# Norm sums, sums' engine, bias rows, last stores and last output chunk of an encoder trunk

## The chip, the cores and the metric

One core of a Trainium2 chip runs the whole program. The metric is device time in microseconds (us), the median of three runs. Everything is 32-bit float at the interface. The engines are TensorE (PE; PEld is its weight load), VectorE (DVE), ScalarE (ACT), GpSimd (POOL) and SyncE (SP, which issues most transfers). Each has a queue of its own and works it off in order.

## The reference

A trunk of two layers on `x` of 1024 tokens by 1024 features. Layer 0 is chunkwise retention (4 heads), layer 1 is chunked attention (16 heads of 64, each chunk of 64 queries sees itself and 8 chunks before it, with a learned relative bias), and each is followed by a squared-ReLU MLP of width 4096. Cut to what matters:

```python
for i in range(DEPTH):                       # 2
    hn = _rmsnorm(h, mix_norm_g[i])          # h * rsqrt(mean(h*h) + eps) * gain
    h = h + (_retention if i == 0 else _chunk_attention)(hn, ...)
    u = relu(_rmsnorm(h, mlp_norm_g[i]) @ mlp_w1[i])
    h = h + (u * u) @ mlp_w2[i]
return _rmsnorm(h, final_norm_g)
# attention, per chunk and head
s = q @ k.T * scale + bias[max(rel, -256) + 256]
o = softmax(s) @ v                            # then o @ att_w_out
```

## The kernel before, in words

The activations `h` stay in the core's memory, turned: 8 tiles of 128 features by 1024 tokens, worked in two halves (`hf`) of 512 tokens. Every full-precision product is made of three single-pass ones: an operand is split into a rounded high half (ScalarE) and the rest as a low half (VectorE), by `split` (L133), and `mm3` (L159) issues high x high, low x high, high x low.

**Norms.** A projection runs on `h` times the gain, not yet divided by the root mean square; that factor is applied to the outputs. `Norm.square` (L203) squares a tile on ScalarE and GpSimd adds it to one of two accumulators `acc`. `Norm.finish` (L219) then splits `acc` into `ah` and `al` on VectorE, lets TensorE sum over the partitions with matmuls against two columns of ones (`pc`), computes the inverse root (`col_rsqrt`), and, where the factor is wanted along the columns, writes it 128 wide on VectorE (`wide`), has TensorE turn it and ScalarE copy it to `rB`.

**Seven products.** The up projections of both MLPs and the projections of the attention layer (`Seven`, 16, 12 and 16 jobs of 256 output columns) use seven block products in place of eight (Strassen-Winograd). `XNorm.block` (L284) makes the operands of products 1, 2, 5, 6 while the projection before still runs; `late` (L304) makes those of 3, 7, 4 during the first products. `Group.sums` (L331) makes four sums of weight blocks on GpSimd per job, `make` splits a weight into halves. `Seven.go` (L392) issues a list of steps (job, product): products 1, 2, 5, 6 of jobs 0 and 1, then 3, 3, 7, 4, 7, 4, then the jobs one after the other. Each step gets its weights ready two steps ahead; behind each step an evacuation on VectorE or ScalarE follows and `done` scales an output by `rB` and stores it. Hooks by step number hang in the norm (`finish` of half 0 behind step 0, of half 1 behind step 1) and the late operands (`spread`, L418). The text calls the first 14 steps a start.

**Attention layer.** `qk_job` (L959) scales a tile of queries or keys, splits it and stores four pieces through SyncE (L974); `bias_rows` (L1022) builds, behind step 15, a table of the bias rows, all from ScalarE's queue, and sends 16 rows, each to 64 rows of a skewed copy (L1034 to L1036). The core loads heads (`load_q`, `load_k`, `load_b`, L1049 to L1069) and runs 64 units (head, group of queries) as a software pipeline of scores, softmax, transposes and values. Beside it a `Filler` issues a group of the output projection per unit: `att_out` (L1079) takes chunks of 256 rows of the output weights, three of them beside the core, the fourth behind it (L1230), where `XNorm.block` follows each finished tile.

**Orders.** The framework lays out each engine's queue from the order in the code and from what is ready in its plan; pools of tiles whose memory is reused wait tile by tile. At the start of the program (L666 to L683) the squares of both halves, two projections, `finish` of half 0 and the first rotary products follow one another; half 1 comes inside the second pair. At its end (L1259 to L1285) the final norm's squares, `finish` and the stores of the output are interleaved with the last products.

```python
def finish(self, psp, hf, row=True):
    ah = self.own("ah", F32R)
    al = self.own("al", F32R)
    split(self.acc[hf], ah, al, "dve")
...
hooks[0].append(lambda: fin(0))
hooks[1].append(lambda: fin(1))
```

## Time and profile before

| | |
|---|---|
| median of 3 runs | 2930.65 us (2927.86 to 2933.59) |
| the profiled execution, its own time | 2939.48 us |
| its span, first to last instruction | 2937.7 us |
| mean granted TensorE clock over the span | 0.972 |
| busy: TensorE, VectorE, ScalarE, GpSimd | 95%, 54%, 36%, 23% |
| memory traffic | 313 MB, 107 GB/s |

The rows of the next section come from one profiled execution. Times are from the span's start. A wait row reads "who, at which line, for whom: us in total, times, longest". A group row reads "line, engine, operation, output and inputs, shapes, count, then busy us, mean ns of one, then idle time of the engine just before". A timeline row reads "start, duration, engine, line, operation, output and inputs", with the idle time before it in brackets; "ACTq" and "SPq" are transfers that the engine issues.

### The profile page before, as it was taken

How to read it: one execution, taken by the hardware profiler on the slowest of the kernel's cores; microseconds unless marked ns; L12 is line 12 of the kernel's file. 1: busy time of each engine (PE TensorE's matmuls, PEld its weight loads, DVE VectorE, ACT ScalarE, POOL GpSimd, SP SyncE). 2: the span in 40 equal slices, each digit the busy share in tenths (PEclk: the TensorE clock that was granted, in tenths of full speed). 3: DMA queues.
4: the chain of work that ended last, by engine and by line, in shares of the span. 5: the costliest groups of instructions: out<-in, count | busy, mean ns of one | idle time of the engine just before them, and what ended most of it. 6: DMA issues, size and time to landing. Idle time of an engine off the chain costs nothing.

```text
span 2937.7 us, 34754 instructions
## 1 busy us (share of the span) xinstructions
PE 2783.1 (95%) x12762; PEld 2283.6 (78%) x12762; DVE 1584.8 (54%) x2659; ACT 1065.0 (36%) x1888; POOL 678.6 (23%) x591
## 2 busy tenths in 40 slices
PE   7999999889998999999999789979997999999998
PEld 6888888778886788878888568768985788788887
DVE  4331123366557744454555856668889544545544
ACT  4101221233324444431223434468874444422222
POOL 4220000032214422200001522245545322100002
PEclk9999999989999999999999899989998999999999
DMA  4322333343211233242331255586530323333321
GB/s 123 107 94 78 108 111 99 130 136 108 80 51 29 86 112 111 97 162 82 108 104 43 58 173 160 143 212 157 146 88 22 125 102 114 126 118 108 108 83 58
DMA packets 247771, 313.04 MB, mean 107 GB/s; under 512 B 14664, under 2 KB 170416, under 8 KB 245552
## 3 DMA queue, kind: packets, MB, share of 16 engines
q1 hardware_dynamic: 246048, 307.87, 33.9%
q10 hardware_dynamic: 1552, 2.95, 0.3%
q8 instruction: 100, 1.64, 0.2%
q14 instruction: 71, 0.58, 0.1%
HBM read 222.64 MB, written 90.74 MB: 107 GB/s over the span
## 4 chain that ended last, share of the span: by engine, by line
PE 81%; DVE 9%; ACT 4%; DMA 2%; issue 2%; POOL 2%; ACTq 0%; SPq 0%; POOLq 0%; DVEq 0%
PE ps L165 17%; PE ps L164 17%; PE ps L166 17%; PE pA L164 5%; PE pA L165 5%; PE pA L166 5%; PE pC L166 2%; PE pC L165 2%; PE pC L164 2%; PE po L1170 1%; DVE xl L140 1%; PE pt L1158 1%; PE pB L165 1%; PE pB L166 1%; PE pB L164 1%
## 5 line engine op out<-in xcount | busy, mean ns | idle before, releaser
L482 DVE TENSOR_TENSOR h<-ps,h 128x512 f32<-128x512 f32 x368 | 252.5, 688 | 341.6 <-PE ps L166 340.7
L136 ACT CAST whi<-wraw 128x1024 fp32r<-128x1024 f32 x132 | 138.8, 1052 | 767.4 <-PE ps L165 580.4
L165 PE MATMUL ps<-ul,whi 128*128 128x512 f32 x960 | 374.2, 390 | 1.9 <-DVE ul L140 1.7
L166 PE MATMUL ps<-uh,wlo 128*128 128x512 f32 x960 | 373.5, 389 | 0.0
L164 PE MATMUL ps<-uh,whi 128*128 128x512 f32 x960 | 373.0, 389 | 0.0
L164 PE MATMUL pA<-xh,wh 128*128 128x512 f32 x704 | 282.3, 406 | 17.0 <-ACT xh L136 5.6
L166 PE MATMUL pA<-xh,wl 128*128 128x512 f32 x704 | 281.1, 400 | 15.9 <-DVE wl L140 15.9
L165 PE MATMUL pA<-xl,wh 128*128 128x512 f32 x704 | 281.0, 399 | 5.0 <-DVE xl L140 5.0
L212 POOL TENSOR_TENSOR acc<-acc,sq 128x512 f32<-128x512 f32 x70 | 99.1, 1417 | 768.5 <-ACT sq L211 767.4
L140 DVE TENSOR_TENSOR wlo<-wraw,whi 128x1024 fp32r<-128x1024 f32 x125 | 159.2, 1274 | 171.0 <-ACT whi L136 171.0
L165 PEld LDWEIGHTS ps<-ul,whi 128*128 128x128 f32 x960 | 180.2, 188 | 42.1 <-DVE ul L140 4.5
L164 PEld LDWEIGHTS ps<-uh,whi 128*128 128x128 f32 x960 | 180.0, 188 | 37.5 <-ACT uh L136 0.4
L166 PEld LDWEIGHTS ps<-uh,wlo 128*128 128x128 f32 x960 | 180.2, 188 | 37.1
L164 PE MATMUL ps<-hhi,whi 128*128 128x512 f32 x512 | 204.5, 399 | 2.6 <-ACT whi L136 1.8
L165 PE MATMUL ps<-hlo,whi 128*128 128x512 f32 x512 | 204.3, 399 | 0.0
L166 PE MATMUL ps<-hhi,wlo 128*128 128x512 f32 x512 | 203.8, 398 | 0.0
L164 PEld LDWEIGHTS pA<-xh,wh 128*128 128x128 f32 x704 | 135.6, 193 | 59.4 <-DVE c L413 15.8
L140 DVE TENSOR_TENSOR wl<-wS,wh 128x512 fp32r<-128x512 f32 x176 | 142.5, 810 | 67.0 <-ACT wh L136 66.1
L166 PEld LDWEIGHTS pA<-xh,wl 128*128 128x128 f32 x704 | 135.0, 192 | 47.6 <-DVE wl L140 18.9
L165 PEld LDWEIGHTS pA<-xl,wh 128*128 128x128 f32 x704 | 135.5, 193 | 33.3 <-DVE xl L140 5.8
L340 POOL TENSOR_TENSOR wS<-wr 128x512 f32<-128x512 f32 x44 | 59.9, 1361 | 415.2 <-DVE wl L140 393.1
L136 ACT CAST wh<-wS 128x512 fp32r<-128x512 f32 x176 | 109.4, 621 | 123.0 <-PE pB L165 58.2
(227 smaller groups left out, 6084.9 us busy)
## 6 DMA issues: line engine op xcount, KB each, us to landing
wr<-in_mlp_w_dram SPq DMA_DIRECT2D x32, 1024.0 KB, 5.4
uD<-c SPq DMA_DIRECT2D x128, 256.0 KB, 2.0
wraw<-in_mlp_w_dram SPq DMA_DIRECT2D x64, 512.0 KB, 3.4
xr<-uD SPq DMA_DIRECT2D x128, 256.0 KB, 3.1
wraw<-in_ret_w_in_dram SPq DMA_DIRECT2D x48, 512.0 KB, 4.1
kk<-kA SPq DMA_DIRECT2D x32, 512.0 KB, 8.3
wr<-in_att_w_in_dram SPq DMA_DIRECT2D x12, 1024.0 KB, 5.3
vS<-t SPq DMA_DIRECT2D x32, 256.0 KB, 2.0
```

The costliest lines, as they stand in the source:

```text
L136: nc.scalar.copy(out=hi, in_=src)
L140: eng.tensor_tensor(out=lo, in0=src, in1=hi.bitcast(F32), op=ALU.subtract)
L164: nc.tensor.matmul(ps, lhsT=lh, rhs=rh, start=start, stop=False, skip_group_check=more)
L165: nc.tensor.matmul(ps, lhsT=lh, rhs=rl, start=False, stop=False, skip_group_check=more)
L166: nc.tensor.matmul(ps, lhsT=ll, rhs=rh, start=False, stop=stop, skip_group_check=more)
L212: nc.gpsimd.tensor_tensor(out=self.acc[hf], in0=self.acc[hf], in1=sq, op=ALU.add)
L340: nc.gpsimd.tensor_tensor(out=t, in0=a[1, 0], in1=a[0, 0], op=ALU.subtract)
L482: nc.vector.tensor_tensor(out=hv, in0=ps, in1=hv, op=ALU.add)
L1158: nc.tensor.transpose(pt[:, c - done:c - done + P], pr[:, (kb - k0) * P:(kb - k0 + 1) * P], ident)
L1170: nc.tensor.matmul(po[:, oc:oc + n], lhsT=T[hd, "v"][:, kb, :], rhs=t[:, off[kb]:off[kb] + n], start=i == 0, stop=i == len(seq) - 1)
```

## The change

The squares are added on VectorE, and so are the four sums of weight blocks. `finish` is cut in two: `sums` takes the sum over the partitions straight from the 32-bit accumulator with 4 matmuls a half, without splits, and `turn` makes `rB`, with ScalarE writing the wide rows. In `Seven.go` both `sums` stand behind step 2 and both `turn` behind step 4; outputs of earlier steps are kept and handed to `done` after step 4. The operand of product 7 is made from the tiles by ScalarE and one VectorE instruction, that of product 4 by two VectorE instructions. At the program's start `sums` of both halves come ahead of the second pair of weights, `turn` and the first rotary products inside it. The 16 bias rows leave ScalarE's queue: SyncE sends one behind every second step from 24 to 54. The stores of the last query and the last key job (32 of them) are issued by GpSimd. The output projection is cut into two chunks of 256 rows beside the attention core and one of 512 rows behind it, instead of three and one of 256.

```diff
@@ -209,31 +209,29 @@
                 nc.scalar.activation(sq, hv, AF.Square)
-                nc.gpsimd.tensor_tensor(out=self.acc[hf], in0=self.acc[hf], in1=sq, op=ALU.add)
+                nc.vector.tensor_tensor(out=self.acc[hf], in0=self.acc[hf], in1=sq, op=ALU.add)
         def block(self, m, hf):
...
             self.square(m, hf)
-        def finish(self, psp, hf, row=True):
-
-            ah = self.own("ah", F32R)
-            al = self.own("al", F32R)
-            split(self.acc[hf], ah, al, "dve")
+        def sums(self, psp, hf):
+
             pc = psp.tile([P, HT], F32, name="pc", tag="ps")
             for t in range(4):
-                for i, z in enumerate((ah, al)):
-                    nc.tensor.matmul(pc[:, 2 * t:2 * t + 2], lhsT=z[:, t * P:(t + 1) * P], rhs=ones[:, 0:2], start=i == 0, stop=i == 1)
+                nc.tensor.matmul(pc[:, 2 * t:2 * t + 2], lhsT=self.acc[hf][:, t * P:(t + 1) * P], rhs=ones.bitcast(F32)[:, 0:2], start=True, stop=True)
             col_rsqrt(self.gp, pc, hf)
-            if row:
-                wide = tmp_tile(self.gp, "wide")
-                ps = psp.tile([P, HT], F32, name="pss", tag="ps")
-                for t in range(4):
-                    sl = slice(t * P, (t + 1) * P)
-                    nc.vector.tensor_scalar(out=wide[:, sl], in0=ones.bitcast(F32), scalar1=rcol[:, 4 * hf + t:4 * hf + t + 1], scalar2=None, op0=ALU.mult)
-                    nc.tensor.transpose(ps[:, sl], wide[:, sl], ident)
-                nc.scalar.copy(out=rB[:, hf * HT:(hf + 1) * HT], in_=ps)
+
+        def turn(self, psp, hf):
+
+            wide = tmp_tile(self.gp, "wide")
+            ps = psp.tile([P, HT], F32, name="pss", tag="ps")
+            for t in range(4):
+                sl = slice(t * P, (t + 1) * P)
+                nc.scalar.activation(wide[:, sl], ones.bitcast(F32), AF.Copy, scale=rcol[:, 4 * hf + t:4 * hf + t + 1])
+                nc.tensor.transpose(ps[:, sl], wide[:, sl], ident)
+            nc.scalar.copy(out=rB[:, hf * HT:(hf + 1) * HT], in_=ps)
@@ -308,15 +306,20 @@
                 yield
-            for p, z in ((7, 0), (4, 1)):
-                for j in range(4):
-                    g, b = self.parts(j)
-                    src, q = (b[0][1], 3) if p == 7 else (b[1][0], 6)
-                    t = tmp_tile(gp, "t")
-                    nc.vector.scalar_tensor_tensor(out=t, in0=src, scalar=g[z], in1=x.hi[q][:, j, :].bitcast(F32), op0=ALU.mult, op1=ALU.subtract)
-                    nc.gpsimd.tensor_tensor(out=t, in0=t, in1=x.lo[q][:, j, :].bitcast(F32), op=ALU.subtract)
-                    x.split(p, j, t)
-                    yield
+            for j in range(4):
+                g, b = self.parts(j)
+                b22, t3 = tmp_tile(gp, "b22"), tmp_tile(gp, "t3")
+                nc.scalar.activation(b22, b[1][1], AF.Copy, scale=g[1])
+                nc.vector.scalar_tensor_tensor(out=t3, in0=b[0][1], scalar=g[0], in1=b22, op0=ALU.mult, op1=ALU.subtract)
+                x.split(7, j, t3)
+                yield
+            for j in range(4):
+                g, b = self.parts(j)
+                t4 = tmp_tile(gp, "t4")
+                nc.vector.scalar_tensor_tensor(out=t4, in0=b[1][0], scalar=g[1], in1=x.hi[6][:, j, :].bitcast(F32), op0=ALU.mult, op1=ALU.subtract)
+                nc.vector.tensor_tensor(out=t4, in0=t4, in1=x.lo[6][:, j, :].bitcast(F32), op=ALU.subtract)
+                x.split(4, j, t4)
+                yield
     class Group:
@@ -333,13 +336,13 @@
                 if p == 5:
-                    nc.gpsimd.tensor_tensor(out=t, in0=a[1, 0], in1=a[1, 1], op=ALU.add)
+                    nc.vector.tensor_tensor(out=t, in0=a[1, 0], in1=a[1, 1], op=ALU.add)
                 elif p == 6:
-                    nc.gpsimd.tensor_tensor(out=t, in0=self.s[5], in1=a[0, 0], op=ALU.subtract)
+                    nc.vector.tensor_tensor(out=t, in0=self.s[5], in1=a[0, 0], op=ALU.subtract)
                 elif p == 7:
-                    nc.gpsimd.tensor_tensor(out=t, in0=a[1, 0], in1=a[0, 0], op=ALU.subtract)
+                    nc.vector.tensor_tensor(out=t, in0=a[1, 0], in1=a[0, 0], op=ALU.subtract)
                 else:
-                    nc.gpsimd.tensor_tensor(out=t, in0=a[0, 1], in1=self.s[6], op=ALU.subtract)
+                    nc.vector.tensor_tensor(out=t, in0=a[0, 1], in1=self.s[6], op=ALU.subtract)
         def make(self, p):
@@ -351,7 +354,8 @@
-        AHEAD = 2
+
+        AHEAD, NORM = 2, 4
         def __init__(self, wa, jobs):
@@ -389,10 +393,10 @@
                 self.ready(s)
-        def go(self, wr, psp, gp, x, hooks=None):
+        def go(self, wr, psp, gp, x, hooks):
             self.wr = wr
             names = {1: "A", 2: "B", 5: "C"}
-            held = {}
+            held, pending = {}, []
             for s, (i, p) in enumerate(self.steps):
@@ -411,16 +415,21 @@
                     nc.vector.tensor_tensor(out=t, in0=bank, in1=held[i, {2: 1, 7: 5, 3: 6}[p]], op=ALU.add)
-                    done(*{2: (0, 0), 7: (1, 1), 3: (0, 1)}[p], t)
-                for f in (hooks or {}).get(s, ()):
+                    pending.append((done, *{2: (0, 0), 7: (1, 1), 3: (0, 1)}[p], t))
+                for f in hooks.get(s, ()):
                     f()
-
-    def spread(norm, xb, fin, more=()):
+                if s >= self.NORM:
+                    for f, *z in pending:
+                        f(*z)
+                    pending.clear()
+
+    def spread(norm, xb, psp, more=()):
         gen = norm.late(xb)
         hooks = {s: [] for s in range(12)}
-        hooks[0].append(lambda: fin(0))
-        hooks[1].append(lambda: fin(1))
+        for hf in range(2):
+            hooks[2].append(lambda hf=hf: norm.sums(psp, hf))
+            hooks[Seven.NORM].append(lambda hf=hf: norm.turn(psp, hf))
         for i in range(12):
@@ -534,7 +543,7 @@
             psp = pool(st, "psU", None, 2, PSUM)
-            seven.go(wr, psp, norm.gp, norm.x, spread(norm, xb, lambda hf: norm.finish(psp, hf)))
+            seven.go(wr, psp, norm.gp, norm.x, spread(norm, xb, psp))
     SEATS = 13
@@ -669,17 +678,16 @@
             first[1] = [up_group(psp, norm, w, 1) for w in ws]
-            norm.finish(psp, 0)
-            rope_scale(0)
-            rope(0, 0, *first[0])
+            norm.sums(psp, 0)
+            norm.sums(psp, 1)
             for i in range(1, 2 * RH):
...
                     p1, p2 = (up_group(psp, norm, w, hf) for w in ws)
-                    if i == 1 and hf == 0:
-                        norm.finish(psp, 1)
-                        rope_scale(1)
-                        rope(0, 1, *first[1])
+                    if i == 1:
+                        norm.turn(psp, hf)
+                        rope_scale(hf)
+                        rope(0, hf, *first[hf])
                     rope(i, hf, p1, p2)
@@ -971,7 +979,7 @@
                 for y, part in ((0, hi.bitcast(F32)), (1, t)):
-                    DMA.dma_start(out=dst[p][a, y, :, sl] if which == 0 else dst[p][a, :, y, sl], in_=part[rows, :])
+                    (nc.gpsimd if i == 3 else DMA).dma_start(out=dst[p][a, y, :, sl] if which == 0 else dst[p][a, :, y, sl], in_=part[rows, :])
         c0 = which * D + i * 2 * P
@@ -1031,11 +1039,14 @@
             nc.scalar.dma_start(out=extd[:, 639:640], in_=ext2[0:AH, 320:321])
-            for i in range(AH):
-                row = extd[i:i + 1, :]
-                nc.scalar.dma_start(out=skew[i][:, 0:640], in_=bass.AP(tensor=row.tensor, offset=row.offset, ap=[[0, DH], [1, 640]]))
-
-        seven.go(wr, psp, gp, norm.x, spread(norm, xb, lambda hf: norm.finish(psp, hf), [(15, bias_rows)]))
+
+        def skew_row(i):
+            row = extd[i:i + 1, :]
+            DMA.dma_start(out=skew[i][:, 0:640], in_=bass.AP(tensor=row.tensor, offset=row.offset, ap=[[0, DH], [1, 640]]))
+
+        more = [(15, bias_rows)] + [(24 + 2 * i, lambda i=i: skew_row(i)) for i in range(AH)]
+
+        seven.go(wr, psp, gp, norm.x, spread(norm, xb, psp, more))
     xs.close()
@@ -1073,12 +1084,11 @@
             load_b(hd)
-        NC = 2
         obuf = {}
-        def att_out(box, c, lo_eng="dve"):
-            return down(box, I["att_w_out"][0, c * NC * P:(c + 1) * NC * P, :], NC,
-                        lambda kb, hf: tuple(t[:, hf * HT:(hf + 1) * HT] for t in obuf[c * NC + kb]), "act", lo_eng)
+        def att_out(box, c0, n, lo_eng="dve"):
+            return down(box, I["att_w_out"][0, c0 * P:(c0 + n) * P, :], n,
+                        lambda kb, hf: tuple(t[:, hf * HT:(hf + 1) * HT] for t in obuf[c0 + kb]), "act", lo_eng)
         with ExitStack() as st:
@@ -1198,8 +1208,8 @@
                     j = i - L2 + 1
-                    if j % (8 * NC) == 0 and j < n:
-                        fill.add(att_out(dict(psp=pF), j // (8 * NC) - 1, "pool"))
+                    if j in (16, 32):
+                        fill.add(att_out(dict(psp=pF), j // 8 - 2, 2, "pool"))
                 if L1 <= i < n + L1:
@@ -1217,7 +1227,7 @@
             norm = XNorm(3, gp, xa, xt, 4)
-            run_tail(att_out(dict(psp=psp, norm=norm), NP // NC - 1), 8, seven)
+            run_tail(att_out(dict(psp=psp, norm=norm), NP - 4, 4), 8, seven)
         rs.close()
@@ -1267,10 +1277,10 @@
                             if m == 1:
-                                fin.finish(psp, 0, row=False)
+                                fin.sums(psp, 0)
                             elif m >= 3 and m < 7:
                                 leave(m - 3)
-                fin.finish(psp, 1, row=False)
+                fin.sums(psp, 1)
                 for t in range(4, NB):
```

## Rows read from the trace of the kernel before

**Rows 1.** The page's first part: busy us, share of the span, instructions.
```profile
PE 2783.1 (95%) x12762; PEld 2283.6 (78%) x12762; DVE 1584.8 (54%) x2659; ACT 1065.0 (36%) x1888; POOL 678.6 (23%) x591
```
**Rows 2.** Stretches: length, busy us (count) PE PEld DVE ACT POOL, clock, DMA, GB/s.
```profile
0.00:75.00 75.00, 58.56 (x263) 47.34 (x264) 35.57 (x70) 31.75 (x51) 33.79 (x31) 0.91 0.41 126
935.80:1003.30 67.50, 52.36 (x198) 40.43 (x197) 59.06 (x77) 28.23 (x52) 35.28 (x23) 0.82 0.20 57
1010.00:1235.00 225.00, 225.00 (x984) 183.47 (x983) 107.80 (x164) 96.07 (x165) 62.58 (x46) 1.00 0.33 111
1622.40:1695.70 73.30, 51.53 (x204) 38.71 (x204) 62.91 (x86) 29.40 (x52) 35.40 (x23) 0.88 0.27 72
1700.00:1735.00 35.00, 23.84 (x101) 18.38 (x101) 13.86 (x26) 8.36 (x18) 6.46 (x5) 0.80 0.60 184
...
2193.90:2216.40 22.50, 22.05 (x98) 17.95 (x98) 19.42 (x25) 12.74 (x23) 9.37 (x7) 1.00 0.15 48
2216.40:2296.40 80.00, 55.60 (x201) 41.71 (x202) 69.11 (x91) 36.49 (x64) 41.62 (x27) 0.77 0.20 63
```
**Rows 3.** Waits of TensorE, whole span; `pss` in 0 to 75 alone.
```profile
PE pc L227 <- DVE ah L138: 24.3, 4, 9.8
...
PE pS L1129 <- DMA kk<-kA: 14.6, 1, 14.6
PE pB L164 <- ACT wh L136: 11.4, 2, 11.2
...
PE pss L235 <- DVE wide L234: 7.5, 2, 5.8
```
**Rows 4.** Groups of VectorE, 930 to 1004; the last row 2300 to 2500.
```profile
L140 DVE TENSOR_TENSOR wl<-wS,wh 128x512 fp32r<-128x512 f32 x9 | 10.3, 1144 | 0.1
L140 DVE TENSOR_TENSOR xl<-t,xh 128x512 fp32r<-128x512 f32 x8 | 10.0, 1245 | 2.9 <-ACT xh L136 2.4
L316 DVE SCALAR_TENSOR_TENSOR t<-h,gall,xh 128x512 f32<-128x512 f32 x8 | 7.9, 1004 | 0.0
L266 DVE SCALAR_TENSOR_TENSOR xl<-h,gall,xh 128x512 fp32r<-128x512 f32 x6 | 7.6, 1276 | 1.8 <-ACT xh L265 1.8
...
L140 DVE TENSOR_TENSOR al<-acc,ah 128x512 fp32r<-128x512 f32 x2 | 2.4, 1224 | 0.0
L234 DVE TENSOR_SCALAR wide<-ones,rcol 128x128 f32<-128x128 f32 x8 | 1.8, 283 | 0.1
...
L140 DVE TENSOR_TENSOR wl<-wr,wh 128x512 fp32r<-128x512 f32 x31 | 21.3, 687 | 22.0 <-ACT wh L136 22.0
```
**Rows 5.** A group of GpSimd, the whole span.
```profile
L212 POOL TENSOR_TENSOR acc<-acc,sq 128x512 f32<-128x512 f32 x70 | 99.1, 1417 | 768.5 <-ACT sq L211 767.4
```
**Rows 6.** Timeline of ScalarE, 1713 to 1724.
```profile
1713.57 10.21 ACTq L1036 DMA_DIRECT2D skew<-extd  x16
1723.82 0.37 ACT L989 CAST vt<-pv 128x256 fp32r<-128x256 f32 x1 [15.76 <-DMA skew<-extd]
```
**Rows 7.** Timeline of SyncE, 1916.5 to 1917.9.
```profile
1916.66 0.59 SPq L974 DMA_DIRECT2D kA<-c  x1
1917.36 0.53 SPq L1052 DMA_DIRECT2D qh<-qA  x1
```
**Rows 8.** The page's transfers: engine, count, KB each, us to landing.
```profile
kk<-kA SPq DMA_DIRECT2D x32, 512.0 KB, 8.3
```
**Rows 9.** Stretches, the units' sums (L1178) alone: length, DVE busy (count), clock, DMA.
```profile
1945.00:1993.00 48.00, 5.88 (x14) 1.00 0.77 194
2010.00:2180.00 170.00, 16.83 (x40) 1.00 0.54 140
```
**Rows 10.** Timeline, 2918 to 2929: GpSimd's last square, VectorE's read of the sums.
```profile
2922.26 1.50 POOL L212 TENSOR_TENSOR acc<-acc,sq 128x512 f32<-128x512 f32 x1 [1.86 <-ACT sq L211]
...
2927.44 0.16 DVE L182 TENSOR_SCALAR vc<-pc 128x4 f32<-128x4 f32 x1 [2.49 <-PE pc L227]
```
**Rows 11.** Stretch 43 to 45, the sum matmuls (L227) alone: length, PE, PEld, clock.
```profile
43.00:45.00 2.00, 0.95 (x8) 1.04 (x8) 1.00 0.80 238
```

## The prediction

> **What bounds the kernel now.** The page's first part comes first: TensorE is busy 95% of the span, VectorE 54% [rows 1]. So the question is where TensorE stands still or runs at its lower level. The table of stretches tells that [rows 2]. In a steady stretch (1010 to 1235) 984 matmuls take 225 us, 0.229 us each, at a granted clock of 1.00. One product of a projection (4 blocks of 3 matmuls) is then 2.75 us, a job of seven 19.2 us. The three starts of a seven-product projection look different. Each start is the 14 products of the first two jobs, 168 matmuls, 38.5 us at the steady pace, and they took 67.5, 73.3 and 80.0 us with clocks of 0.82, 0.88 and 0.77. VectorE is busy 59.1 of 67.5, 62.9 of 73.3 and 69.1 of 80.0 us there: in these stretches it, not TensorE, is the bound. The waits of TensorE name the rest [rows 3]: 24.3 us for the split of the norm sum (`ah`), 7.5 us in the first stage for `wide`, 11.4 us for a weight half behind ScalarE, 14.6 us for the first keys of the attention core. GpSimd's own work is short, but VectorE's instructions beside it are long: a low half made from a GpSimd sum means 1144 ns in the first start, one made straight from the loaded weights in a steady stretch 687 ns [rows 4].
>
> **The change part by part.** The sum is made against the profiled execution (2939.48 us, span 2937.7); the median of the runs, 2930.65, is 8.8 us below it, and I take the sum off the median.
>
> *Additions on VectorE, in the starts.* In the first start GpSimd has 23 instructions [rows 2]: 11 weight sums, 4 squares, 8 subtractions of the late operands. Of the subtractions four disappear (product 7 now takes ScalarE's `b22`), four move. So 19 x 0.69 = 13.1 us come to VectorE. What leaves: the stretching, (1144-687)x9 + (1245-687)x8 + (1004-687)x8 + (1276-687)x6 = 14.7 us, if no GpSimd instruction runs beside it; the splits of the norm sum, 2.4 us for `al`, and 1.8 us for `wide`, which goes to ScalarE [rows 4]. 59.1 + 13.1 - 14.7 - 4.2 = 53.3 us. VectorE idled 8.4 us of that start; the ends are none of this idle time left and all of it, so 53.3 to 61.7 us. I take half, 57.5: the idle time came partly from GpSimd's answers, but ScalarE's are still awaited. First start: **-10 us** (-6 to -14). The second by the same 5.8 us on VectorE: 57.1 busy, half of 10.4 idle, 62.3: **-11 us** (-6 to -16). The wait for `ah` (9.8 us in the longest case, part of the 24.3) lies inside these sums and isn't counted again: the sums now stand behind the third product, when the squares are done, and the output of product 2 is held back to step 4. What is late next is VectorE's own queue: late operands and weight halves.
>
> *Squares before a start* are hidden by TensorE's down projection, one group of 12 matmuls (2.75 us) each; they cost 14 x 0.69 = 9.7 us of VectorE there against the stretching that leaves. Zero, between -2 and +3 us per start, is inside the ends above. *The weight sums in the steady stretch*: 46 GpSimd instructions become 46 x 0.69 = 31.7 us more on VectorE, 107.8 + 31.7 = 140 of 225 us [rows 2]. The free 38% hide them, and sums are issued two products ahead; if that cover goes, see the second rival. The pending outputs hold one 128x512 tile for three products, behind which nothing waits.
>
> *First stage.* The norm sums of both halves run ahead of the next weights and the rows are turned a projection later. The 7.5 us of waits for `wide` go [rows 3]; I take **-7 us**, since the rotary products now pile up behind `turn` (-4 to -9, the upper end for part of the 0.91 clock).
>
> *Norm sums without splits*: 4 f32 matmuls a half instead of 8. Eight took 0.95 us [rows 11]; no row shows an f32 one that isn't a transpose. Bounds: half of it, and four times that half, -0.5 to +0.95 us a half; I take 0, as the starts are VectorE's. The page FP8 and Floating Point Precision of the Trainium skill (TensorE Precision Notes) says that true FP32 takes four passes through the array, which speaks against this part; by it each half would cost the 0.95 us more, on the path in three halves (two in the first stage, one at the end), and the sum would be 59 instead of 62.
>
> *Bias rows.* ScalarE is taken for 16.4 us: it waits for the row table to land and then issues 16 transfers in 10.21 us, and the next conversion starts at 1723.82 [rows 6]. TensorE waits 11.4 us for it [rows 3]. The stretch 1700 to 1735 has 101 matmuls, at most 23.1 us of work [rows 2]: loss 11.9 us. The three table stores stay on ScalarE, but it no longer waits for them to land. On SyncE each row costs some 0.6 us, one in two products (5.5 us), steps 24 to 54, long after the table landed; the weight load and the stores behind it are later by 0.6 us at most, with whole jobs of slack. **-12 us** (-10 to -14).
>
> *Last stores on GpSimd's queue.* Now the loads of the first heads stand behind the last key stores on SyncE: the last is issued at 1916.66, the first load at 1917.36 [rows 7], and the keys take 8.3 us to land [rows 8], so TensorE waits 14.6 us. With the stores gone from SyncE, queries and keys of head 0 can go when their memory is free, products before the end; a part overlaps the last weights and waits for them. What remains is between nothing and one full landing, 8.3 us; I take 5.5, nearer the landing, as the bias tile comes last: **-9 us** (-6 to -13). GpSimd's price isn't in the trace: bounds 0.59 us (SyncE's issue [rows 7]) and 1.42 us (a 128x512 instruction of its own [rows 5]), 32 x that = 19 to 45 us, against 38.5 us of the last two jobs in which GpSimd now has nothing else. At the upper end it lags 7 us, and behind its stores stand the bias tiles' edges and the scaling of the first softmax rows; that takes the term to -3.
>
> *Last output chunk 512 deep.* One filler chunk leaves the attention core. 14 units without filler took 48 us, 3.43 each; 40 units with it 170 us, 4.25 each [rows 9]. Sixteen units lose 0.82 us each; the last four have no scores beside them, so 12 x 0.82 = 10 us (5 to 13). The chunk's 96 matmuls come back at the end: that projection grows from 96 to 192 matmuls, 43.9 us instead of 22.5. In return its blocks finish in fours instead of in two bursts, as ahead of the first start. So 22.5 + 80.0 becomes 43.9 + 57.5 = 101.4, 1 us less. Together **-11 us** (+4 to -17).
>
> *End.* From the last square's addition (2922.26, 1.50 us on GpSimd) to the sums read at 2927.44 [rows 10]: the addition is 0.8 us shorter and the split goes: **-2 us** (0 to -4).
>
> Sum: 10 + 11 + 7 + 12 + 9 + 11 + 2 = 62 us. 2930.65 - 62 = **2869 us**. All upper ends give -87, 2844; all lower ones -25 (6 + 6 + 4 + 10 + 3 - 4 + 0), 2906.
>
> **The rivals.** *VectorE's order eats the starts.* In each start its queue keeps all its idle time and the third start gains nothing net: 6 + 6 + 7 + 12 + 9 + 0 + 2 = 42, about 2889. For it: it is the bound there, and each square must wait for ScalarE. Against: the stretched rows. 0.2.
> *Sums in VectorE's queue block the weights everywhere (slower).* A sum waiting for its weights to land, or for one of three buffers, now holds up every low half and output behind it; GpSimd could wait alone. Place: each of the 44 jobs. It decides from 62/44 = 1.4 us of TensorE wait a job; at 2 us it gives 88 - 62 = +26, 2957. Against: 38% of VectorE free and sums two products ahead. 0.05.
> *GpSimd's stores hold the attention core.* If a store costs the upper price or more, the entry gains nothing: 53, 2878. The page SBUF — State Buffer of the Trainium skill (the "DVE blocks DMA" trap) says that a transfer issued from GpSimd stands while VectorE works in a two-port mode, since its descriptors can't be written; no transfer from GpSimd is in this trace. 0.12.
> *Clock and waits feed each other.* If the starts run without long waits, the 0.77 to 0.88 clocks go too and VectorE idles less: 2848. For it: clock 1.00 in every stretch without waits. 0.13.
> *The change does little of what it says*, the instructions being laid out so that the sums stay where VectorE is late: all lower ends, 2906. 0.05.
>
> **How the numbers follow.** My forecast has 0.45. All cases but one are below 2925, the bound at which 0.2%, about what a measurement of this kernel can tell from no change, begins. Faster 0.93, within 0.2% 0.02, slower 0.05. The range 2840 to 2902 holds the forecast with its terms mixed, the first, third and fourth rival; outside are the slower rival, the one that does little, and a few combinations.
>
> **What would show it.** Right: no TensorE wait of over 2 us for the norm sums; the starts at 55 to 63 us, with mean VectorE low halves near 0.69 us; no gap near the bias rows; some 5 us ahead of the core; heads 12 to 15 nearer 14 us than 17. Wrong: a steady job over 19.5 us with waits for `wl` or `wS`; GpSimd's queue still issuing stores when the first scores are done; the third start as long as before with 44 us ahead of it.

## The result and the profile after

The changed kernel takes **2858.34 us** (median of 4 runs, 2852.08 to 2860.36), the kernel before 2929.26 beside it (4 runs): ratio 0.9754, 95% interval 0.9733 to 0.9776, 71 us less. Forecast were 62 less, 2869, in a range of 2840 to 2902. The profiled execution of the changed kernel took 2858.98 us (span 2857.2), close to its median. That of before lies 10 us above the median beside it, so a difference of the two traces says some 10 us too much.

The page's first part, for [rows 1]:

```profile
PE 2763.7 (97%) x12762; PEld 2272.0 (80%) x12762; DVE 1624.3 (57%) x2851; ACT 1080.7 (38%) x1932; POOL 305.1 (11%) x351
```

GpSimd has 240 instructions fewer and VectorE 192 more, yet VectorE's busy time grew by only 39.5 us. Next the stretches, for [rows 2] (columns as there): the first stage, the first start, a steady stretch, the second start, the rest of that projection, the last output projection, the third start. From here on a start is counted exactly, from its first matmul to the first one of the third job; so counted, the three starts before were 66.4, 70.7 and 78.1 us long.

```profile
0.00:75.00 75.00, 65.48 (x313) 53.65 (x314) 41.43 (x75) 35.26 (x60) 16.69 (x17) 1.00 0.46 141
924.10:976.10 52.00, 45.77 (x193) 36.11 (x192) 42.86 (x77) 29.31 (x57) 0.00 (x0) 0.90 0.29 91
1000.00:1225.00 225.00, 225.00 (x985) 183.65 (x984) 137.39 (x212) 95.34 (x163) 0.00 (x0) 1.00 0.31 106
1596.50:1651.60 55.10, 47.38 (x193) 36.85 (x192) 45.95 (x83) 29.18 (x57) 0.00 (x0) 0.88 0.33 89
1651.60:1854.80 203.20, 201.77 (x904) 162.50 (x903) 141.94 (x237) 83.76 (x157) 15.87 (x27) 1.00 0.61 175
2120.00:2163.80 43.80, 43.80 (x196) 36.29 (x196) 35.28 (x54) 24.09 (x40) 0.73 (x1) 1.00 0.09 25
2163.80:2218.30 54.50, 47.57 (x194) 37.77 (x192) 44.01 (x78) 31.24 (x59) 0.00 (x0) 0.87 0.27 87
```

To be seen: the first stage holds 50 more matmuls in its first 75 us and has its full clock; each start is 14 to 24 us shorter; the steady stretch holds the same work with VectorE at 137.39 of 225 us; and in the starts VectorE now has 9 to 10 us without work. The waits of TensorE over the whole span, for [rows 3]:

```profile
...
PE pS L1139 <- DMA kk<-kA: 9.3, 1, 9.3
PE pA L164 <- ACT wh L136: 9.3, 3, 4.1
PE pA L166 <- DVE wl L140: 8.5, 3, 2.9
...
PE pC L164 <- ACT wh L136: 2.3, 3, 1.2
PE pc L223 <- DVE acc L212: 2.3, 1, 2.3
```

The 24.3 us for `ah`, the 7.5 for `wide` and the 11.4 for a weight half are gone. The 2.3 us for a norm sum (`acc`) stand at the program's end, none in a start. What is left in each start is a short wait at product 5 (`pC`) and two at the third job's first product. The groups of VectorE in the first start, for [rows 4]:

```profile
L140 DVE TENSOR_TENSOR wl<-wS,wh 128x512 fp32r<-128x512 f32 x8 | 5.5, 684 | 1.9 <-ACT wh L136 1.9
L140 DVE TENSOR_TENSOR xl<-t,xh 128x512 fp32r<-128x512 f32 x8 | 5.5, 683 | 0.0
L264 DVE SCALAR_TENSOR_TENSOR xl<-h,gall,xh 128x512 fp32r<-128x512 f32 x4 | 3.0, 744 | 0.1
```

They were 1144, 1245 and 1276 ns. The entry to the attention core, for [rows 7, 8]: GpSimd's last store and SyncE's load of the first keys, in the timelines of the two.

```profile
1858.70 0.52 POOL L982 DMA_DIRECT2D kA<-c  x1
```

```profile
1850.08 0.41 SPq L1063 DMA_DIRECT2D qh<-qA  x1
1855.03 1.33 SPq L1069 DMA_DIRECT2D kk<-kA  x2
```

A store costs GpSimd 0.52 us. The queries are loaded before the projection has ended (1854.8); the keys' load waits for the last product, whose memory it takes, and lands 9 us later. And the end, for [rows 10]: the last addition and VectorE's read of the sums, 1.9 us apart, 5.2 before.

```profile
2844.98 0.69 DVE L212 TENSOR_TENSOR acc<-acc,sq 128x512 f32<-128x512 f32 x1 [0.69 <-ACT sq L211]
...
2846.88 0.16 DVE L182 TENSOR_SCALAR vc<-pc 128x4 f32<-128x4 f32 x1 [0.81 <-PE pc L223]
```

### The profile page after: what moved, and what is told of

It reads as the page before. It is cut to its first block, busy times and chain, and to the rows that moved or that the text cites. A ratio compares the mean times of both kernels' runs of the same rounds, so it can differ in the third digit from the quotient of the medians.

```text
span 2857.2 us, 34484 instructions
## 1 busy us (share of the span) xinstructions
PE 2763.7 (97%) x12762; PEld 2272.0 (80%) x12762; DVE 1624.3 (57%) x2851; ACT 1080.7 (38%) x1932; POOL 305.1 (11%) x351
## 4 chain that ended last, share of the span: by engine, by line
PE 86%; DVE 6%; ACT 4%; issue 2%; DMA 1%; POOL 0%; SPq 0%; POOLq 0%; DVEq 0%; ACTq 0%
PE ps L165 18%; PE ps L164 18%; PE ps L166 18%; PE pA L164 6%; PE pA L166 5%; PE pA L165 5%; PE pC L164 3%; PE pC L166 3%; PE pC L165 3%; PE pB L164 1%; PE pB L166 1%; PE pB L165 1%; PE po L1180 1%; PE pt L1168 1%; ACT pr L1148 1%
## 5 line engine op out<-in xcount | busy, mean ns | idle before, releaser
L491 DVE TENSOR_TENSOR h<-ps,h 128x512 f32<-128x512 f32 x352 | 242.2, 689 | 343.3 <-PE ps L166 342.3
L164 PE MATMUL pC<-xh,wh 128*128 128x512 f32 x352 | 139.8, 397 | 2.3 <-ACT wh L136 2.3
L166 PE MATMUL pC<-xh,wl 128*128 128x512 f32 x352 | 140.4, 399 | 0.6 <-DVE wl L140 0.6
L140 DVE TENSOR_TENSOR wl<-wS,wh 128x512 fp32r<-128x512 f32 x176 | 120.9, 687 | 33.6 <-ACT wh L136 33.0
```

The source lines that it names most:

```text
L140: eng.tensor_tensor(out=lo, in0=src, in1=hi.bitcast(F32), op=ALU.subtract)
L164: nc.tensor.matmul(ps, lhsT=lh, rhs=rh, start=start, stop=False, skip_group_check=more)
L166: nc.tensor.matmul(ps, lhsT=ll, rhs=rh, start=False, stop=stop, skip_group_check=more)
L491: nc.vector.tensor_tensor(out=hv, in0=ps, in1=hv, op=ALU.add)
```

## The experiments

All but the first take the changed kernel and undo or move one part, e5, e11 and e12 two; each was timed in turn with the kernel before (2929 to 2930 us).

| run | median us | ratio to before, 95% | the three starts, us |
|---|---|---|---|
| the change | 2858.34 | 0.9754 (0.9733 to 0.9776) | 52.0, 55.1, 54.5 |
| e2: all sums on GpSimd | 2906.64 | 0.9919 (0.9904 to 0.9934) | 65.2, 69.6, 65.4 |
| e3: norm sums early | 2848.20 | 0.9719 (0.9704 to 0.9733) | 48.7, 50.5, 49.4 |
| e4: four output chunks | 2856.05 | 0.9749 (0.9733 to 0.9765) | 52.3, 53.1, 63.2 |
| e5: e2 with e3 | 2903.70 | 0.9906 (0.9892 to 0.9921) | 65.1, 68.3, 65.5 |
| e6: bias rows on ScalarE | 2868.67 | 0.9789 (0.9775 to 0.9804) | 52.2, 53.2, 54.7 |
| e7: last stores on SyncE | 2863.37 | 0.9772 (0.9755 to 0.9788) | 52.3, 53.9, 50.9 |
| e8: weight sums on GpSimd | 2861.48 | 0.9764 (0.9749 to 0.9779) | 55.2, 54.2, 53.8 |
| e9: late operands on GpSimd | 2864.53 | 0.9777 (0.9763 to 0.9792) | 55.2, 55.7, 58.0 |
| e10: squares on GpSimd | 2888.23 | 0.9857 (0.9839 to 0.9874) | 58.5, 63.8, 62.0 |
| e11: e3 with e4 | 2850.09 | 0.9731 (0.9715 to 0.9746) | 48.7, 50.5, 62.3 |
| e12: e11, late operands sooner | 2849.59 | 0.9729 (0.9712 to 0.9745) | 48.7, 52.2, 62.4 |

The intervals of e7, e8 and e9 overlap that of the change, and e8's 3 us are hardly told apart from nothing. Starts whose code is that of the change (e4 but for its third, e6, e7) take 52.0 to 52.3, 53.1 to 55.1 and 50.9 to 54.7 us, so a difference of 2 us in a second start, or 4 in a third, can be spread.

**e1**, the kernel before again.

> The kernel before once more, for a second profile. The profiled execution shown of it was 8.8 us above the median. Theory: those 9 us lie in one place, the first stage or one of the three starts, where the granted clock was low, and the second profile then has a time of 2925 to 2934 with one of these stretches shorter by 6 to 9 us (the first stage's retention marker at 576 to 579 us in place of 584.5, or a start of 60 to 75 us in place of 67.5, 73.3 and 80.0). Rival: the 9 us are spread evenly, every stretch shorter by 0.3%.

2934.08 us, span 2932.3. The first start begins 3.3 us sooner, and no other stage differs by over 1.7 us. The projections of the first stage end at 572.3 us in both; the 3.3 us lie in the retention layer behind them and the rest is spread, so neither text is quite right. For terms of a few us before has two values: first start at 935.8 and 932.5, starts of 66.4 and 65.1, 70.7 and 71.2, 78.1 and 78.8 us.

**e2**, every sum on GpSimd, late operands in their old form.

```
-                nc.vector.tensor_tensor(out=self.acc[hf], in0=self.acc[hf], in1=sq, op=ALU.add)
+                nc.gpsimd.tensor_tensor(out=self.acc[hf], in0=self.acc[hf], in1=sq, op=ALU.add)
...
-                    nc.vector.tensor_tensor(out=t, in0=a[1, 0], in1=a[1, 1], op=ALU.add)
+                    nc.gpsimd.tensor_tensor(out=t, in0=a[1, 0], in1=a[1, 1], op=ALU.add)
```

> The changed kernel with every sum back on GpSimd: weight sums, additions of the squares, and the late operands in their old form. The norm sums keep their place behind the third product. Theory (VectorE beside GpSimd is stretched, and that was most of what the starts cost): VectorE's low halves in the starts are back at 1.1 to 1.25 us, each start is longer by 5 to 9 us, with no wait of TensorE for the norm sums; time 2858 + 15 to 27 = 2873 to 2885. Rival (the place of the norm sums made the gain, the engine of the sums nothing): 2856 to 2864, starts within 2 us of the changed kernel's.

48 us are lost, well over the theory's 27, and the rival falls. The engine of the sums is the largest part of the change. The first start's row shows why the forecast's account of it can't be whole:

```profile
927.60:992.80 65.20, 50.83 (x193) 38.95 (x192) 49.62 (x65) 30.37 (x59) 33.89 (x23) 0.84 0.24 73
```

VectorE is busy 49.62 of 65.20 us. It has 15.6 us to spare, and the start is slow all the same.

**e3**, norm sums and turning behind the first and second product; `NORM = 1` also ends the holding back of early outputs.

```
-        AHEAD, NORM = 2, 4
+        AHEAD, NORM = 2, 1
...
-            hooks[2].append(lambda hf=hf: norm.sums(psp, hf))
-            hooks[Seven.NORM].append(lambda hf=hf: norm.turn(psp, hf))
+            hooks[hf].append(lambda hf=hf: (norm.sums(psp, hf), norm.turn(psp, hf)))
```

> The changed kernel with the norm sums and their turning back behind the first and the second product of a start, and the outputs no longer held back to step 4. All sums stay on VectorE. Theory (VectorE's load decides, the place only when it is late): TensorE waits 2 to 5 us for the last square's sum in each of three starts, part of it taken from the waits that come later anyway; time 2858 + 3 to 12 = 2861 to 2870. Rival (the place made the gain of the starts): waits of 6 to 10 us a start, granted clock in the starts back at 0.77 to 0.88, time 2878 to 2888.

Both fall: it is **10 us faster** than the change. TensorE waits for no norm sum in a start; with the squares on VectorE the last one is added at about the time when the first product ends. The stretches of the three starts:

```profile
922.50:971.20 48.70, 43.89 (x193) 35.27 (x193) 42.59 (x77) 29.43 (x57) 0.00 (x0) 0.93 0.31 97
1590.90:1641.40 50.50, 44.24 (x194) 34.45 (x193) 46.09 (x84) 29.71 (x57) 0.00 (x0) 0.93 0.36 98
2154.90:2204.30 49.40, 44.30 (x194) 34.62 (x193) 43.45 (x78) 31.54 (x59) 0.00 (x0) 0.97 0.31 96
```

They are 3.3, 4.6 and 5.1 us shorter, at a higher clock. The place behind the third product, on which the change builds, costs time. Where, the changed kernel's own timeline of TensorE and the clock of two pieces of it show:

```profile
930.42 0.50 PE L164 MATMUL pC<-xh,wh 128*128 128x512 f32 x1 [0.63 <-ACT wh L136]
930.75 0.40 PE L165 MATMUL pC<-xl,wh 128*128 128x512 f32 x1
930.99 1.84 PE L223 MATMUL pc<-ones,acc 128*128 128x2 f32 x16
932.69 0.69 PE L166 MATMUL pC<-xh,wl 128*128 128x512 f32 x1
```

```profile
930.00:932.70 2.70, 2.28 (x19) 2.19 (x19) 2.70 (x5) 0.98 (x2) 0.00 (x0) 1.00 0.93 285
932.70:936.20 3.50, 3.50 (x11) 2.73 (x11) 2.24 (x7) 0.72 (x2) 0.00 (x0) 0.51 0.16 57
```

TensorE waited 0.63 us for a weight half, did all sixteen records of the norm sums in a row, and then ran 3.5 us at 0.51, the 1.2 GHz level. In e3 the sums come eight at a time, no wait stands beside them, and the clock is 1.00 there. In the first start the 0.6 us of wait and about 1.7 us of half clock (half of 3.5) are most of the 3.3. The clock does not fall there each time: in the second start, with 0.45 us of wait, it fell in the changed kernel and in e7 (55.1 and 53.9 us), and stayed at 1.00 in e4 and e6 (53.1 and 53.2 us). e3 has 50.5 there, so the late place costs something without the clock too. With four chunks the same edit is worth 6 us (e11 against e4). The outputs no longer held back are part of it and were not tried alone.

**e4**, four chunks of 256 rows again.

```
-                    if j in (16, 32):
-                        fill.add(att_out(dict(psp=pF), j // 8 - 2, 2, "pool"))
+                    if j % (8 * NC) == 0 and j < n:
+                        fill.add(att_out(dict(psp=pF), j // (8 * NC) - 1, "pool"))
```

> The changed kernel with the attention output again in four chunks of 256 rows, three of them as filler in the attention core. Theory: heads 12 to 15 go back from 14 to 17 us each (+10 to +12 us in the core), the projection behind it is 21.4 us shorter, but its blocks finish in two bursts and the third start is longer by some 21 us again; time 2858 + 9 to 14 = 2867 to 2872. Rival (the filler ran in gaps that TensorE has in the core anyway, and with the sums on VectorE the bursts cost little): 2858 - 5 to + 3.

The rival's time: 2 us below the change, inside both intervals. From the trace: the core (first to last scores) takes 254.9 us, 245.5 in the change; the projection behind it is 19.1 us shorter, and the third start 8.7 us longer.

```profile
2128.00:2150.30 22.30, 21.14 (x94) 17.18 (x93) 18.80 (x32) 12.42 (x22) 0.74 (x1) 1.00 0.16 48
2150.30:2213.50 63.20, 48.90 (x193) 37.63 (x194) 56.34 (x99) 39.78 (x74) 0.00 (x0) 0.84 0.24 75
```

Two bursts of blocks still crowd VectorE at that start (56.34 busy), but with the sums on it the start is 63 us and not 78.

**e5**, both of e2 and e3.

> Every sum on GpSimd and the norm sums behind the first and second product, as in the kernel before; the rest as changed. The run with sums on GpSimd and norm sums behind the third product had 2906.6, the changed kernel with early norm sums 2848.2. Theory A (the place behind the third product costs by itself, whatever engine makes the sums): starts of 60 to 63 us in place of 65 to 70, time 2906 - 6 to 15 = 2891 to 2900. Theory B (it is right for slow sums and wrong for quick ones: with GpSimd's squares the early norm sum waits 6 to 10 us a start, as it did before): starts of 66 to 78 us, waits for the last square's sum of 15 us or more in all, time 2906 + 3 to 25 = 2910 to 2931.

Between the two texts: 3 us below e2. With slow sums the place is worth nearly nothing either way; a wait goes from one product to another. With quick sums the early place is better by 10.

**e6**, the sixteen bias rows in one go on ScalarE.

```
+            for i in range(AH):
+                skew_row(i)
...
-            DMA.dma_start(out=skew[i][:, 0:640], in_=bass.AP(tensor=row.tensor, offset=row.offset, ap=[[0, DH], [1, 640]]))
+            nc.scalar.dma_start(out=skew[i][:, 0:640], in_=bass.AP(tensor=row.tensor, offset=row.offset, ap=[[0, DH], [1, 640]]))
```

> The changed kernel with the sixteen bias rows sent by ScalarE in one go again. Theory: ScalarE stands for 16 us, TensorE waits 10 to 12 us for a weight half and loses its full clock for some us; time 2858 + 10 to 16 = 2868 to 2874, all of it in the second stage of projections. Rival (with its conversions earlier now, ScalarE has slack for it): below + 5, 2858 to 2863.

The theory, at its lower end: 10.3 us, with a wait shorter than its 10 to 12. ScalarE's timeline and TensorE's wait are those of [rows 6], 13.15 us in place of 15.76 and 8.7 in place of 11.4:

```profile
1660.57 13.26 ACTq L1047 DMA_DIRECT2D skew<-extd  x15
1673.87 0.37 ACT L997 CAST vt<-pv 128x256 fp32r<-128x256 f32 x1 [13.15 <-DMA skew<-extd]
```

```profile
PE pA L164 <- ACT wh L136: 8.7, 1, 8.7
```

**e7**, the last stores on SyncE.

```
-                    (nc.gpsimd if i == 3 else DMA).dma_start(
+                    DMA.dma_start(
```

> The changed kernel with the stores of the last two projection jobs on SyncE's queue again. Theory: the loads of the first heads stand behind the last stores, the wait for the first keys goes from 9.3 back to about 14.6 us: + 5, 2862 to 2865. Rival 1 (what I forecast, 9 us from this part): + 8 to 12, 2866 to 2870. Rival 2 (the loads wait for their memory, not for the queue): within 2 us of the changed kernel.

The theory: 5.0 us. The timeline of SyncE is that of [rows 7], and the wait for the first keys is 15.3 us, 9.3 in the change.

```profile
1859.80 0.59 SPq L982 DMA_DIRECT2D kA<-c  x1
1860.43 0.59 SPq L1063 DMA_DIRECT2D qh<-qA  x1
1861.12 1.11 SPq L1069 DMA_DIRECT2D kk<-kA  x2
```

**e8, e9, e10** take the three kinds of sums back to GpSimd one at a time, the late operands (e9) in their old form.

> The changed kernel with the weight sums alone on GpSimd; squares and late operands stay on VectorE. All sums on GpSimd cost 48 us. Theory A (instructions of GpSimd beside VectorE stretch it, so the cost goes by their number: 11 of 23 in a start): starts of 57 to 61 us, + 15 to 28, 2873 to 2886. Theory B (the squares and the late operands make it, since TensorE waits for their results, and weight sums two products ahead are free): + 0 to 8, 2858 to 2866.

> The changed kernel with the late operands alone in their old form (eight subtractions of GpSimd in each start, each between two instructions of VectorE on the way to an operand); squares and weight sums stay on VectorE. All three groups on GpSimd cost 48 us, the weight sums alone 3. Theory A (the way VectorE, GpSimd, ScalarE, VectorE of a late operand is the cost): starts of 59 to 66 us, time 2858 + 24 to 42 = 2882 to 2900. Theory B (the squares are the cost: late norm sums and late early operands): + 0 to 8, 2858 to 2866.

> The changed kernel with the additions of the squares alone on GpSimd. Theory A (as above): + 3 to 10 in all, of it 2 to 3 at the end, where the last addition is 0.8 us longer, and 1 to 3 in the first stage; 2861 to 2868. Theory B: starts of 60 us or more, + 30 to 45, 2888 to 2903.

Theory B three times: 3, 6 and **30 us**. (In e10 two starts of three pass the 60 us it asked for, and its time is the lower end.) In the first start of e8 VectorE is stretched, as its group of low halves shows, and little is lost by it:

```profile
L140 DVE TENSOR_TENSOR wl<-wS,wh 128x512 fp32r<-128x512 f32 x8 | 7.2, 904 | 3.5 <-ACT wh L136 3.2
```

So it isn't stretching as such; it is where it falls. In e10 it falls, among other places, on the last 24 us ahead of the start. There, per group of matmuls (2.75 us), VectorE adds the residual, forms an early operand for ScalarE and takes its low half. The changed kernel and then e10, each in the 24.1 us that end with its start, first as stretches and then as groups of VectorE:

```profile
900.00:924.10 24.10, 24.10 (x108) 19.98 (x107) 22.23 (x35) 13.64 (x22) 0.00 (x0) 1.00 0.00 1
```

```profile
905.30:929.40 24.10, 24.10 (x108) 19.93 (x108) 18.54 (x21) 10.78 (x17) 10.16 (x8) 1.00 0.00 1
```

```profile
L295 DVE SCALAR_TENSOR_TENSOR xr<-h,gall,xr 128x512 f32<-128x512 f32 x2 | 1.5, 750 | 0.0
```

```profile
L140 DVE TENSOR_TENSOR xl<-xr,xh 128x512 fp32r<-128x512 f32 x6 | 5.6, 935 | 2.1 <-ACT xh L136 2.0
L491 DVE TENSOR_TENSOR h<-ps,h 128x512 f32<-128x512 f32 x8 | 5.4, 679 | 0.0
L295 DVE SCALAR_TENSOR_TENSOR xr<-h,gall,xr 128x512 f32<-128x512 f32 x2 | 3.2, 1604 | 0.1
L264 DVE SCALAR_TENSOR_TENSOR xl<-h,gall,xh 128x512 fp32r<-128x512 f32 x2 | 2.7, 1332 | 2.7 <-ACT xh L263 2.7
```

With the squares VectorE does 35 instructions, ten of them squares; without them it does 21, and not the other 25, and waits for ScalarE most of its idle time. The operands' `xr` is on the way VectorE, ScalarE, VectorE, and with squares beside them these instructions (L295, L298, L264) take 1.7 to 2.1 times as long in the mean; the residual additions (`h`), with one input from PSUM, keep their 679 ns. The Trainium skill's page GPSIMD Engine Reference (Key points) says just this, that GpSimd shares its way into SBUF with VectorE and that instructions with two SBUF inputs contend; the rows agree. How one falls on the other, in e10's timelines of VectorE and GpSimd:

```profile
917.64 1.86 DVE L295 SCALAR_TENSOR_TENSOR xr<-h,gall,xr 128x512 f32<-128x512 f32 x1
```

```profile
917.66 1.29 POOL L212 TENSOR_TENSOR acc<-acc,sq 128x512 f32<-128x512 f32 x1 [0.49 <-ACT sq L211]
```

VectorE's queue then stands back when the start begins. In the first start TensorE's second product waits for a residual addition. It begins 6.6 us after the start does, in the changed kernel 0.3 us after it:

```profile
936.76 0.80 PE L164 MATMUL pB<-xh,wh 128*128 128x512 f32 x1 [4.44 <-DVE h L491]
```

In the second and the third start of e10 TensorE waits 8.3 us each at product 5, for a weight half:

```profile
PE pC L164 <- ACT wh L136: 17.6, 3, 8.3
```

ScalarE makes that half from a weight sum. VectorE's queue reaches the sum 12.7 us after the second start begins (1607.5), in the changed kernel 4.7 us after it (1596.5). e10's row, then the changed kernel's:

```profile
1620.19 0.68 DVE L339 TENSOR_TENSOR wS<-wr 128x512 f32<-128x512 f32 x1
```

```profile
1601.23 0.69 DVE L339 TENSOR_TENSOR wS<-wr 128x512 f32<-128x512 f32 x1
```

In no start of e10 does TensorE wait for GpSimd's additions as such, so the time is not a wait for late norm sums. That the stretching sets VectorE back, and not another order of its queue without the squares, is read from these rows; no run tells the two apart.

In e10 the three starts are longer by 6.5, 8.7 and 7.5 us, the first start begins 5.3 us later and what follows the third start takes 3.0 us more: 31 us, of which the other stages give back 1.4. The kernel before has the same rows ahead of its first start (`xr` 1608 ns).

**e11, e12**, towards a faster version: early norm sums with four chunks, and then each late operand one product sooner.

```
-            hooks[1 + (i * 3) // 4].append(lambda: next(gen))
+            hooks[(i * 3) // 4].append(lambda: next(gen))
```

> The kernel with early norm sums on VectorE (2848.2), and the attention output in four chunks of 256 rows. Theory (the last chunk's depth is worth nothing: core + 9.3, projection - 19.1, third start + 9): 2845 to 2850. Rival (early norm sums and two bursts meet in VectorE's queue): third start over 12 us longer, 2852 to 2858.

> The same as the run before it, and each late operand issued one product sooner in a start. Theory (the 5 us for which TensorE waits ahead of the third job in each start are late operands that stand too far back in VectorE's queue, which has 8 us without work in a start): 3 to 9 us below the run before it, 2838 to 2846. Rival (an operand sooner holds back a weight half or an output as long): within 2 us of it.

e11 isn't told apart from e3 by its time (2850.09); its third start is 12.9 us longer than e3's, as the rival had it. e12 is e11 within half a microsecond, the rival's case: an operand issued sooner only trades places. That VectorE's free time there is mostly waits for ScalarE, as in the changed kernel's groups, would account for it, but was not tried. The best version measured is **e3**, 2848.2 us.

## Why the prediction was right, and where it was wrong

The time, the side and the range hold, and 62 us against 71 looks close. By its steps it is less so.

**Squares before a start, forecast 0: the step that failed.** It called them hidden by TensorE's down projection, with +3 us a start at worst. e10 measures 30 us for the squares, 23 of them in the three starts. TensorE's groups hid GpSimd's time, but VectorE falls behind there, and it is what the start waits for. The forecast set the stretching ahead of a start against the additions' own time and put zero; it counted the stretched rows [rows 4] inside the starts alone.

**First and second start, -10 and -11.** Measured -13 to -14 and about -16: right side, at the upper end, by another way. The sum gave 53.3 us of work for VectorE in the first start; the row has 42.86. Of the 10 us between, about 5 are seven instructions that VectorE no longer brings into the start (three of the four squares, four of the work ahead of it). About 4 are stretching that the sum had left out: low halves of loaded weights (868 to 685 ns), outputs (865 to 686 ns) and the small instructions of the inverse root (648 to 158 ns). The weight sums and the late operands, 15 of the 19 instructions it counted as added, are worth 3 and 6 us alone (e8, e9). All three kinds together are worth 48 (e2), more than 3 + 6 + 30.

**The place of the norm sums** had no term of its own; the forecast took it for granted. It costs 10 us (e3), 6 with four chunks (e11 against e4).

**Last output chunk, -11: wrong.** Core -10 held (-9.4, e4). The output projection grew by 19.1, near the 21.4 counted. But the third start's 80.0 to 57.5 was put down to the finer blocks; the blocks are worth 8.7 and the rest came with the other parts. The term is about 0 (+2 by the medians, +1 by the stages).

**First stage, -7.** -11.5, beyond the upper end of 9: its projections end at 572.3 us in both profiles of before and at 560.8 in the changed kernel's. The waits for `wide` are gone, as forecast. The other runs with the squares on VectorE have 560.1 to 563.4 there, the three with them on GpSimd (e2, e5, e10) 566.8 to 567.3, so 3 to 7 us of it are the squares'.

**Bias rows, -12.** 10.3 in e6. With slow sums they seem to cost more: outside its start that projection has 840 matmuls at 262 ns each before and 243 in e5, 16 us, and the bias rows are the largest change there.

**Entry, -9.** 5.0 (e7). GpSimd's price, 0.52 us, was below the lower bound, so the third rival didn't come. But 9.3 us of wait are left, not 5.5: the load couldn't start before the last product's memory was free, and bias rows, values and stores move beside it. The Trainium skill's page SBUF — State Buffer (the "DVE blocks DMA" trap) says that a transfer issued by GpSimd stands while VectorE works in a two-port mode. No run here shows that: the last store is issued at 1858.70, 5.8 us ahead of the first scores, and the stores land in 2.6 to 3.9 us in the median, in 2.3 to 2.4 where SyncE issued them before.

**Weight sums in the steady stretch, 0.** Right: 985 matmuls in 225 us, and e8 changes nothing there. The slower rival has no place.

**Norm sums in f32, 0.** Right: a half takes 0.92 us (16 records for both in 1.84), eight split ones took 0.95 [rows 11]. By the four passes in the Trainium skill's page FP8 and Floating Point Precision (TensorE Precision Notes) it would have been 1.9; the trace doesn't show that, and the measurement decides.

**End, -2.** -2.5 to -3.4 by the two profiles of before, from the last residual addition to the end; 2.4 to 3.3 of it lie between the square's addition and the read.

The runs, set in a row from before to the change: all but the engine and the place of the sums, -26 (e5, 2903.7); the engine, -55 (e3, 2848.2); the place, +10 (2858.3). That 62 came near 71 is in part luck: what the squares gave beyond the forecast, and what the chunk, the place and the entry took from it (11, 10 and 4 us), nearly met. The first stage's new order and the norm sums without splits weren't tried alone.

## What to carry to other kernels

Before a helper engine's work is called hidden, look at what the other engine does beside it: instructions on GpSimd that cost nothing of their own made VectorE's up to twice as long in the very stretch whose results the start waits for. When a late result is made early, its place should be tried again; the late slot was meant as a remedy for slow sums, and even with them it gained nothing (e2 against e5). And a gain of a stage that two parts of a change both touch is counted once, at the part that a run alone shows.

## What was not expected of the hardware

A VectorE instruction of two inputs, 0.75 us alone, took 1.86 us with one GpSimd addition of 1.29 us beside it: 1.1 us of delay, nearly the whole of the other's length. A norm sum in f32 shows two records per matmul, 0.115 us each, and costs what two matmuls of its split parts cost. The granted clock fell to 0.51 for 3.5 us after no more than 0.63 us of wait and sixteen two-column records; with eight in a row and no wait (0.95 us) it stayed at 1.00. Sixteen records behind a short wait do not bring it down each time. In the second start five runs have the same 0.44 to 0.45 us of wait ahead of them: the clock then fell in the changed kernel and e7, and stayed at 1.00 in e4, e6 and e9. The 3 us behind them, in the changed kernel and then in e4:

```profile
1605.00:1608.00 3.00, 3.00 (x9) 2.38 (x9) 2.14 (x6) 0.73 (x2) 0.00 (x0) 0.54 0.04 13
```

```profile
1603.30:1606.30 3.00, 3.00 (x15) 2.46 (x15) 2.16 (x7) 1.23 (x4) 0.00 (x0) 1.00 0.05 16
```

What decides was not tried.
